# Gate matrix of a product-key expert layer: low and high gate parts accumulated in PSUM, evicted by ScalarE, weight low parts moved from GpSimd to VectorE

## Chip, core and metric

The kernel runs on one core of one Trainium2 chip. The metric is the device time of one execution in microseconds (us). A profile is one further execution under the hardware profiler; its span runs from the first to the last instruction.

## What is computed

Two transformer blocks act on 256 tokens of width 1024. The change lies in the second block's last layer, an expert layer with product keys (`peer_ffn` in the reference). Per token and head (8 heads), the top 16 of 128 scores are taken on each of two key sets, the 256 sums of pairs are ranked again, and 16 experts out of 16384 (128 x 128) remain, with softmax gates:

```
best, pos = lax.top_k(cand, PEER_TOPK)
idx = jnp.take_along_axis(cand_idx, pos, axis=-1)
g = jax.nn.softmax(best, axis=-1)
act = jax.nn.gelu(jnp.einsum('td,thkd->thk', xc, expert_u[idx]), approximate=False)
w = (g * act).astype(h.dtype)
return jnp.einsum('thk,thkd->td', w, expert_v[idx])
```

The kernel gathers nothing. It computes the activation of all 16384 experts for all tokens, multiplies by a gate matrix that is zero for experts not chosen, and multiplies by all of `expert_v`. An expert is numbered 128 i + j: i is the partition of a tile, j counts the tiles.

## The kernel before, in words

**Weights.** Every weight tile (128 x 1024, float32, 512 KB) comes by a DMA on SP's queue into `raw`; ScalarE copies it to a rounded high part `hi` (L158, L141), and VectorE or GpSimd subtracts to get the low part `lo` (L159). `plan` (from L434) lists the tiles in the order of use and says with `by` which engine subtracts: "v" is VectorE, "g" is GpSimd. Before, all 128 `eu` tiles are "g", all 128 `ev` tiles "v". `ahead(2)` keeps two tiles ready: after the matmuls of tile u, tile u+2 is fetched and split. There are three buffers each of `raw`, `hi` and `lo`.

**Two halves.** The 128 values of j are done in two halves of 64 (`JA`). In each half `experts_u` (L1698) runs 64 units; a unit is one `eu` tile: 24 matmuls of 128 x 256 (L303), 16 with `hi`, then 8 with `lo`. Every second unit, ScalarE takes a pair of activations out of PSUM (`act<-bd`, Gelu). Then `experts_v` (L1784) runs 64 `ev` tiles with matmuls of 512 columns (L1795 to L1797). `prep` (L1775) multiplies a pair of activation tiles by the gates (L1778), and ScalarE and VectorE split the result into `eh` and `el` ahead of those.

**Gates.** `gates3` (L1720) builds the gate matrix `Gt` beside `experts_u`: 32 steps of 8 tokens in each half. A step makes on VectorE a one-hot `oi` of i (L1736, 128 x 1024 in float16), a one-hot `eqj` of j (L1737, 128 x 512), and `eqj` times the gate's high and low float16 parts (`jg`, L1739, two multiplies of 128 x 512). On TensorE, for the step before, 8 matmuls (L1750, one per token, `oi` stationary, 128 moving columns: 64 of the high part, 64 of the low) fill two PSUM banks; VectorE adds the two parts with a reduce per bank (L1752) into `Gt`. In the first half, `second` (L1630) precedes the gates: the second ranking on VectorE, then for each of four (token half, key set) pairs a selection (L1678 to L1681: is_equal, multiply, reduce over 16), and two groups of transposes (L1687) with the casts to `IT`, `JT`, `GHL`.

**Order.** All engines run their instructions in program order. `weave` (L397) writes the order: after unit u of `experts_u`, it issues `CA[u]` steps of the side work in the first half (`second`, then `gates3`), `CB[u]` in the second. What is left over runs after the last unit. A gate step issues its one-hots, then the matmuls of the step before, then their eviction.

```
def prefetch():
    ...
    A(hi[:, :width], raw[:, :width], AF.Copy)
    (V if by == "v" else G).tensor_tensor(lo[:, :width], raw[:, :width], hi[:, :width].bitcast(F32), op=OP.subtract)

for i, _ in enumerate(main):
    steps(side, counts[i] if i < len(counts) else 0)
run(side)
```

Of the kernel before, what the change touches and what calls it, by code (L numbers as in the profile page):

```python
# [10 lines left out]
F16 = mybir.dt.float16  # L11
I32 = mybir.dt.int32
U32 = mybir.dt.uint32
AF = mybir.ActivationFunctionType
OP = mybir.AluOpType
# [80 lines left out]
OUTS = (4, 6, 5, 7, 2, 3, 0, 1)  # L96
JOBS = ('hf', 'gq', 'hq', 'gk', 'gv', 'lqk', 'v5', 'v2', 'sm', 'hg', 'lg', 'z', 'fq', 'fk')
LAG = (1, 1)
CA = [0] * 14 + [1] * 8 + [0, 0, 1, 0] + [1, 0] * 5 + [1, 1] + [1, 1, 2, 1] * 7
CB = [0] * 2 + [1, 0] * 28 + [1] * 6  # L100

BY_V = (0, 1)
# [9 lines left out]
def _emit(ctx, tc, I, out):  # L112
# [12 lines left out]
    def bank(tag="m"):  # L125
        if tag == "d":
            turn_["i"] += 1
            tag = turn_["d"][turn_["i"] % len(turn_["d"])]
        tag = AS.get(tag, tag)
        return ps.tile([128, 512], F32, tag=tag, name="b" + tag, bufs=BANKS[tag])  # L130
# [5 lines left out]
    def A(o, i, f, **kw):  # L136
        t = tables.get(f)
        if t and t != table[0]:
            S.preload_act_table_set(t)
            table[0] = t  # L140
        S.activation(o, i, f, **kw)  # L141
# [6 lines left out]
    def plan(*items, by="v"):  # L148
        order.extend((n, i, w, by) for n, i, w in items)
# [293 lines left out]
    plan(*[("w_out2", i, 1024) for i in range(4, 8)], by=B2)  # L443
    plan(*[("w_query", i, 1024) for i in range(16)], by="g")
    for lo_, hi_ in ((0, JA), (JA, 128)):
        plan(*[("eu", i, 1024) for i in range(lo_, hi_)], by="g")
        plan(*[("ev", i, 1024) for i in range(lo_, hi_)])

    R2 = R[:, None, :].to_broadcast([128, 2, 256])
# [1097 lines left out]

    IT = big.tile([128, 256, 2], F16)
    JT = big.tile([128, 256, 2], F16)
    GHL = big.tile([128, 2, 256, 2], F16)  # L1550
    tk = ExitStack()
    kp = tk.enter_context(tc.tile_pool(name="topk", bufs=1))
    ktmp = tk.enter_context(tc.tile_pool(name="ktmp", bufs=2))
# [76 lines left out]
    def second():  # L1630
        best = ktmp.tile([128, 2, 8, 16], F32, tag="best", name="best", bufs=1)
        pos = ktmp.tile([128, 2, 8, 16], U32, tag="pos", name="pos", bufs=1)
        for t in range(2):
            cd = ktmp.tile([128, 8, 112], F32, tag="cd", name="cd", bufs=1)
            v1, v2 = kv[:, t, 0], kv[:, t, 1]
            V.tensor_tensor(cd[:, :, 0:64].rearrange("p h (a b) -> p h a b", a=4),
                            v1[:, :, 0:4, None].to_broadcast([128, 8, 4, 16]),
                            v2[:, :, None, :].to_broadcast([128, 8, 4, 16]), op=OP.add)
            V.tensor_tensor(cd[:, :, 64:112].rearrange("p h (a b) -> p h a b", a=12),
                            v1[:, :, 4:16, None].to_broadcast([128, 8, 12, 4]),  # L1640
                            v2[:, :, None, 0:4].to_broadcast([128, 8, 12, 4]), op=OP.add)
            for h in range(0, 8, 2):
                top16(112, *((cd[:, i], best[:, t, i], pos[:, t, i]) for i in (h, h + 1)))
                yield

        ab = ktmp.tile([128, 4, 256], U32, tag="ab", name="ab", bufs=1)
        pf_ = pos.rearrange("p t h k -> p (t h k)")
        ge = ktmp.tile([128, 256], U32, tag="ge", name="ge", bufs=1)
        V.tensor_scalar(ab[:, 0], pf_, 4, None, op0=OP.logical_shift_right)
        V.tensor_scalar(ab[:, 1], pf_, 15, None, op0=OP.bitwise_and)  # L1650
        V.tensor_scalar(ab[:, 2], pf_, 2, None, op0=OP.logical_shift_right)
        V.tensor_scalar(ab[:, 3], pf_, 3, None, op0=OP.bitwise_and)
        V.tensor_scalar(ge, pf_, 6, None, op0=OP.logical_shift_right)
        abf = ktmp.tile([128, 4, 256], F32, tag="abf", name="abf", bufs=1)
        V.tensor_copy(abf, ab)
        V.tensor_scalar(abf[:, 2], abf[:, 2], 12.0, None, op0=OP.subtract)
        for i in range(2):
            V.copy_predicated(abf[:, i], ge, abf[:, 2 + i])
        abh = ktmp.tile([128, 2, 2, 8, 16], F16, tag="abh", name="abh", bufs=1)
        V.tensor_copy(abh.rearrange("p i t h k -> p i (t h k)"), abf[:, 0:2])  # L1660
        yield

        sel = ktmp.tile([128, 3, 2, 128], F32, tag="sel", name="sel", bufs=1)
        gg = sel[:, 2].rearrange("p t (h k) -> p (t h) k", h=8)
        bb = best.rearrange("p t h k -> p (t h) k")
        V.tensor_tensor(gg, bb, bb[:, :, 0:1].to_broadcast([128, 16, 16]), op=OP.subtract)
        A(gg, gg, AF.Exp)
        sm_ = ktmp.tile([128, 16], F32, tag="smk", name="smk", bufs=1)
        V.tensor_reduce(out=sm_, in_=gg, op=OP.add, axis=AX.X)
        V.reciprocal(sm_, sm_)  # L1670
        V.tensor_tensor(gg, gg, sm_[:, :, None].to_broadcast([128, 16, 16]), op=OP.mult)
        yield
        for t in range(2):
            for i in range(2):
                ixr = ktmp.tile([128, 8, 16, 16], F16, tag="ixr", name="ixr", bufs=2)
                A(ixr, kix[:, t, i, :, :, None].to_broadcast([128, 8, 16, 16]), AF.Copy)
                eq = ktmp.tile([128, 8, 16, 16], F16, tag="eq", name="eq", bufs=2)
                V.tensor_tensor(eq, abh[:, i, t, :, None, :].to_broadcast([128, 8, 16, 16]),  # L1678
                                io16[:, None].to_broadcast([128, 8, 16, 16]), op=OP.is_equal)
                V.tensor_mul(eq, eq, ixr)  # L1680
                V.tensor_reduce(out=sel[:, i, t].rearrange("p (h k) -> p h k", h=8),  # L1681
                                in_=eq.rearrange("p h a k -> p h k a"), op=OP.add, axis=AX.X)
                yield
        for t in range(2):
            p = bank("g")
            for i in range(3):
                PE.transpose(p[:, i * 128:i * 128 + 128], sel[:, i, t], ident)  # L1687
            ts = slice(t * 128, t * 128 + 128)
            two = lambda z: z[:, :, None].to_broadcast([128, 128, 2])
            V.tensor_copy(IT[:, ts], two(p[:, 0:128]))  # L1690
            V.tensor_copy(JT[:, ts], two(p[:, 128:256]))
            gs = ktmp.tile([128, 128], F32, tag="gs", name="gs", bufs=1)
            V.tensor_scalar(gs, p[:, 256:384], 4096.0, None, op0=OP.mult)
            V.tensor_copy(GHL[:, 0, ts], two(gs))
            V.tensor_sub(GHL[:, 1, ts], two(gs), GHL[:, 0, ts])
            yield

    def experts_u(j0, nj):  # L1698
# [12 lines left out]
    box = {}  # L1711
# [8 lines left out]
    def gates3(j0, nj):  # L1720


        Gt, wtmp, row = box["G"], box["w"], box["r"]

        def pairs(z, n):

            return z[:, :, None, :].to_broadcast([128, 8, n, 2])

        def along(n, j=0):
            return row[:, None, j:j + 2 * n].to_broadcast([128, 8, 2 * n]).rearrange("p t (j e) -> p t j e", e=2)  # L1730

        def one_hots(ts):
            oi = wtmp.tile([128, 8, 64, 2], F16, tag="w1", name="oi")
            jg = wtmp.tile([128, 8, 2, nj // 2, 2], F16, tag="w2", name="jg")
            eq = wtmp.tile([128, 8, nj // 2, 2], F16, tag="w3", name="eqj")
            V.tensor_tensor(oi, along(64), pairs(IT[:, ts], 64), op=OP.is_equal)  # L1736
            V.tensor_tensor(eq, along(nj // 2, j0), pairs(JT[:, ts], nj // 2), op=OP.is_equal)  # L1737
            for i in range(2):
                V.tensor_tensor(jg[:, :, i], eq, pairs(GHL[:, i, ts], nj // 2), op=OP.mult)  # L1739
            return ts, oi, jg  # L1740

        prev = None
        for t0 in range(0, 257, 8):
            new = one_hots(slice(t0, t0 + 8)) if t0 < 256 else None
            if prev:
                ts, oi, jg = prev
                for t4 in (0, 4):
                    p = bank("g").rearrange("p (t i j) -> p t i j", t=4, i=2)
                    for t in range(4):
                        PE.matmul(p[:, t, :, :nj], oi[:, t4 + t].rearrange("p a b -> p (a b)"),  # L1750
                                  jg[:, t4 + t].rearrange("p i a b -> p (i a b)"), start=True, stop=True)
                    V.tensor_reduce(out=Gt[:, :nj, ts.start + t4:ts.start + t4 + 4].rearrange("p j t -> p t j"),  # L1752
                                    in_=p.rearrange("p t i j -> p t j i")[:, :, :nj], op=OP.add, axis=AX.X)
            prev = new
            yield

# [18 lines left out]
    def prep(j):  # L1775
        wtmp = box["w"]
        w = act(j)
        V.scalar_tensor_tensor(w, w, 1.0 / 4096, box["G"][:, j:j + 2], op0=OP.mult, op1=OP.mult)  # L1778
        eh = wtmp.tile([128, 2, 256], F32R, tag="w1", name="eh")
        el = wtmp.tile([128, 2, 256], F32R, tag="w2", name="el")  # L1780
        split(w, eh, el)
        W[j] = eh, el
# [194 lines left out]
```

## Time and profile before

| | us |
|---|---|
| median of 3 runs (1574.97 to 1575.82) | 1575.59 |
| the profiled execution | 1573.7 |
| its span, first to last instruction | 1571.9 |
| mean granted TensorE clock | 0.959 |

PE is TensorE's matmuls, PEld its weight loads, DVE is VectorE, ACT ScalarE, POOL GpSimd. A row of instruction groups ends with: busy time, mean ns of one, and the engine's idle time before them with what ended it. An instruction's time on DVE or POOL includes any time in which it had started and was held up. A granted clock of 1.00 is 2.4 GHz, 0.50 is 1.2 GHz. The page cuts the span into 40 slices of 39.3 us and gives the busy share of each in tenths.

### The profile page before, as it was taken

The page shows a single profiled execution, that of the slowest core. Times are in us where ns is not written, and L with a number is a line of the kernel's source. Part 1 is how long each engine was busy: PE and PEld are TensorE (multiplying, and loading weights), DVE is VectorE, ACT ScalarE, POOL GpSimd, SP SyncE. Part 2 cuts the span into 40 slices and gives each one's busy share as a digit, 9 for nine tenths or more (in the row PEclk, how much of TensorE's full clock was granted, in tenths as well). Part 3 has the DMA queues.
Part 4 walks back from the last instruction along what each step waited for, and adds up shares of the span by engine and source line. Part 5 has one row for each costly group of instructions (what it writes and reads, how often), then busy time and mean ns, then how long its engine had stood idle before and what let it go on. Part 6 is the DMA issues. An engine that isn't in the chain of part 4 may idle for free.

```text
span 1571.9 us, 26239 instructions
## 1 busy us (share of the span) xinstructions
PE 1452.1 (92%) x10548; PEld 1323.0 (84%) x10548; DVE 1176.6 (75%) x1912; ACT 708.5 (45%) x986; POOL 582.6 (37%) x247
## 2 busy tenths in 40 slices
PE   7789898999998899979999787799999999999997
PEld 6678767999987788979998677688889999988886
DVE  4666747997783667667938999866667999976665
ACT  5623434665553345435446222244544444444444
POOL 3453212000035444866789444100007888800000
PEclk9989969999999999999999888899999999999999
DMA  6332103566544333454555332266665555556663
GB/s 217 114 94 69 55 15 113 174 200 189 185 140 132 94 95 108 153 170 136 169 183 172 106 94 94 95 189 198 192 197 179 171 172 171 168 174 191 198 194 127
DMA packets 63788, 231.35 MB, mean 147 GB/s; under 512 B 7073, under 2 KB 7602, under 8 KB 63282
## 3 DMA queue, kind: packets, MB, share of 16 engines
q1 hardware_dynamic: 62640, 226.00, 46.6%
q10 hardware_dynamic: 1026, 3.68, 0.6%
q8 instruction: 82, 1.34, 0.3%
q14 instruction: 40, 0.33, 0.1%
HBM read 228.60 MB, written 1.05 MB: 146 GB/s over the span
## 4 chain that ended last, share of the span: by engine, by line
PE 31%; DVE 21%; ACT 0%; issue 0%; DVEq 0%; ACTq 0%
PE bd L303 8%; PE bm L1796 7%; PE bm L1795 7%; PE bm L1797 7%; DVE jg L1739 7%; DVE oi L1736 5%; DVE Gt L1752 4%; DVE eqj L1737 1%; DVE sel L1681 1%; DVE eq L1680 1%; PE bn L1750 1%; DVE lo L159 0%; DVE eq L1678 0%; ACT fy L141 0%; DVE fz L1830 0%
## 5 line engine op out<-in xcount | busy, mean ns | idle before, releaser
L159 POOL TENSOR_TENSOR lo<-raw,hi 128x1024 fp32r<-128x1024 f32 x230 | 575.9, 2512 | 784.1 <-ACT hi L141 725.3
L141 ACT ACTIVATE hi<-raw 128x1024 fp32r<-128x1024 f32 x426 | 448.0, 1055 | 422.4 <-PE bd L303 234.2
L303 PE MATMUL bd<-Xh,hi 128*128 128x256 f32 (+1 forms) x1592 | 413.5, 296 | 14.1 <-ACT Xh L141 7.6
L303 PE MATMUL bd<-Xl,hi 128*128 128x256 f32 (+1 forms) x1592 | 401.7, 288 | 0.7 <-DVE Xl L240 0.7
L303 PEld LDWEIGHTS bd<-Xh,hi 128*128 128x128 f32 (+1 forms) x1592 | 313.2, 197 | 20.1 <-ACT Xh L141 7.6
L303 PEld LDWEIGHTS bd<-Xl,hi 128*128 128x128 f32 (+1 forms) x1592 | 313.0, 197 | 1.7 <-DVE Xl L240 1.0
L159 DVE TENSOR_TENSOR lo<-raw,hi 128x1024 fp32r<-128x1024 f32 x196 | 239.2, 1224 | 82.4 <-ACT hi L141 82.4
L303 PE MATMUL bd<-Xh,lo 128*128 128x256 f32 (+1 forms) x1592 | 223.6, 283 | 0.2 <-POOL lo L159 0.2
L303 PEld LDWEIGHTS bd<-Xh,lo 128*128 128x128 f32 (+1 forms) x1592 | 205.5, 191 | 0.4 <-POOL lo L159 0.4
L1795 PE MATMUL bm<-hi,eh 128*128 128x512 f32 x512 | 200.2, 391 | 3.3 <-ACT eh L141 3.3
L1796 PE MATMUL bm<-hi,el 128*128 128x512 f32 x512 | 200.2, 391 | 0.2 <-DVE el L179 0.2
L1797 PE MATMUL bm<-lo,eh 128*128 128x512 f32 x512 | 199.9, 390 | 0.0
L1739 DVE TENSOR_TENSOR jg<-eqj,GHL 128x512 f16<-128x512 f16 x128 | 130.3, 1059 | 2.2
L1795 PEld LDWEIGHTS bm<-hi,eh 128*128 128x128 f32 x512 | 96.6, 189 | 23.9 <-ACT eh L141 3.7
L1796 PEld LDWEIGHTS bm<-hi,el 128*128 128x128 f32 x512 | 96.5, 189 | 20.9 <-DVE el L179 1.0
L1797 PEld LDWEIGHTS bm<-lo,eh 128*128 128x128 f32 x512 | 96.5, 189 | 20.0
L1736 DVE TENSOR_TENSOR oi<-iorow,IT 128x1024 f16<-128x1024 f16 x64 | 96.4, 1506 | 2.4 <-PE bm L1797 2.0
L141 ACT ACTIVATE eh<-act 128x512 fp32r<-128x512 f32 x64 | 40.4, 632 | 127.0 <-DVE act L1778 127.0
L1752 DVE TENSOR_REDUCE Gt<-bn 128x256 f32<-128x512 f32 x128 | 82.0, 682 | 9.3 <-PE bn L1750 9.1
L179 DVE TENSOR_TENSOR el<-act,eh 128x512 fp32r<-128x512 f32 x64 | 44.3, 693 | 49.3 <-ACT eh L141 49.3
L1750 PE MATMUL bn<-jg,oi 128*128 128x128 f16 x512 | 44.9, 227 | 32.9 <-DVE Gt L1752 32.6
L1750 PEld LDWEIGHTS <-oi 128*128 128x128 f16 x512 | 32.6, 100 | 39.6 <-issue 26.3
(576 smaller groups left out, 2143.4 us busy)
## 6 DMA issues: line engine op xcount, KB each, us to landing
raw<-in_eu SPq DMA_DIRECT2D x128, 512.0 KB, 3.5
raw<-in_ev SPq DMA_DIRECT2D x128, 512.0 KB, 3.7
raw<-in_w_in SPq DMA_DIRECT2D x61, 512.0 KB, 3.6
raw<-in_w_up SPq DMA_DIRECT2D x44, 512.0 KB, 3.6
raw<-in_w_down SPq DMA_DIRECT2D x22, 512.0 KB, 3.7
raw<-in_w_out SPq DMA_DIRECT2D x16, 512.0 KB, 3.5
raw<-in_w_query SPq DMA_DIRECT2D x16, 512.0 KB, 3.5
raw<-in_w_ba SPq DMA_DIRECT2D x4, 512.0 KB, 3.5
```

What stands on the lines that cost most here:

```text
L141: S.activation(o, i, f, **kw)
L159: (V if by == "v" else G).tensor_tensor(lo[:, :width], raw[:, :width], hi[:, :width].bitcast(F32), op=OP.subtract)
L179: V.tensor_tensor(lo, src, hi.bitcast(F32), op=OP.subtract)
L303: PE.matmul(o, w[:, k * 128:k * 128 + M], x[:, k], start=n == 0, stop=n == 23)
L1680: V.tensor_mul(eq, eq, ixr)
L1736: V.tensor_tensor(oi, along(64), pairs(IT[:, ts], 64), op=OP.is_equal)
L1739: V.tensor_tensor(jg[:, :, i], eq, pairs(GHL[:, i, ts], nj // 2), op=OP.mult)
L1750: PE.matmul(p[:, t, :, :nj], oi[:, t4 + t].rearrange("p a b -> p (a b)"), jg[:, t4 + t].rearrange("p i a b -> p (i a b)"), start=True, sto ...
L1752: V.tensor_reduce(out=Gt[:, :nj, ts.start + t4:ts.start + t4 + 4].rearrange("p j t -> p t j"), in_=p.rearrange("p t i j -> p t j i")[:, :, ...
L1795: PE.matmul(o, eh[:, i, ts], v[0][:, n_], start=False, stop=False, skip_group_check=True)
L1796: PE.matmul(o, el[:, i, ts], v[0][:, n_], start=False, stop=False, skip_group_check=True)
L1797: PE.matmul(o, eh[:, i, ts], v[1][:, n_], start=False, stop=last and j + i == nj - 1, skip_group_check=True)
```

## The change

Four edits. (1) `eu` tiles 26 to 63 get their low part from VectorE. (2) The selection's reduce becomes four adds that halve the 16 in turn. (3) The two `jg` multiplies become one of 128 x 1024; the gate parts lie side by side per token (`GHL`, `jg` are laid out anew). (4) A gate step has 16 matmuls of 64 columns, two per token that accumulate in the same 64 columns; one PSUM bank holds 8 tokens, and one ScalarE copy evicts it, scaled by 1/4096; `prep` then needs no scale. `CA` brings the softmax step and the gate steps forward: the transposes follow units 34 and 35 instead of 36 and 37, and gate steps follow units 36 to 63 as 1, 1, 1, 1, 2.

```diff
-CA = [0] * 14 + [1] * 8 + [0, 0, 1, 0] + [1, 0] * 5 + [1, 1] + [1, 1, 2, 1] * 7
+CA = [0] * 14 + [1] * 8 + [0, 0, 1, 1] + [1, 0] * 4 + [1, 1] + [1, 1, 1, 1, 2] * 6
+UG = 26
...
-        plan(*[("eu", i, 1024) for i in range(lo_, hi_)], by="g")
+        ug = UG if lo_ == 0 else hi_
+        plan(*[("eu", i, 1024) for i in range(lo_, ug)], by="g")
+        plan(*[("eu", i, 1024) for i in range(ug, hi_)])
...
-    GHL = big.tile([128, 2, 256, 2], F16)
+    GHL = big.tile([128, 256, 2, 2], F16)
...
-                V.tensor_reduce(out=sel[:, i, t].rearrange("p (h k) -> p h k", h=8),
-                                in_=eq.rearrange("p h a k -> p h k a"), op=OP.add, axis=AX.X)
+                for w in (8, 4, 2):
+                    V.tensor_add(eq[:, :, 0:w], eq[:, :, 0:w], eq[:, :, w:2 * w])
+                V.tensor_add(sel[:, i, t].rearrange("p (h k) -> p h k", h=8), eq[:, :, 0], eq[:, :, 1])
...
-            for i in range(2):
-                V.tensor_tensor(jg[:, :, i], eq, pairs(GHL[:, i, ts], nj // 2), op=OP.mult)
+            V.tensor_tensor(jg.rearrange("p (t i) j e -> p t i (j e)", i=2),
+                            eq.rearrange("p t j e -> p t (j e)")[:, :, None].to_broadcast([128, 8, 2, nj]),
+                            pairs(GHL[:, ts].rearrange("p t i e -> p (t i) e"), h), op=OP.mult)
...
-                for t4 in (0, 4):
-                    p = bank("g").rearrange("p (t i j) -> p t i j", t=4, i=2)
-                    for t in range(4):
-                        PE.matmul(p[:, t, :, :nj], oi[:, t4 + t].rearrange("p a b -> p (a b)"),
-                                  jg[:, t4 + t].rearrange("p i a b -> p (i a b)"), start=True, stop=True)
-                    V.tensor_reduce(out=Gt[:, :nj, ts.start + t4:ts.start + t4 + 4].rearrange("p j t -> p t j"),
-                                    in_=p.rearrange("p t i j -> p t j i")[:, :, :nj], op=OP.add, axis=AX.X)
+                p = bank("g").rearrange("p (t j) -> p t j", t=8)
+                for t in range(8):
+                    for i in range(2):
+                        PE.matmul(p[:, t, :nj], oi[:, t].rearrange("p a b -> p (a b)"),
+                                  jg[:, 2 * t + i].rearrange("p a b -> p (a b)"), start=i == 0, stop=i == 1)
+                A(Gt[:, :nj, ts].rearrange("p j t -> p t j"), p[:, :, :nj], AF.Copy, scale=1.0 / 4096)
...
-        V.scalar_tensor_tensor(w, w, 1.0 / 4096, box["G"][:, j:j + 2], op0=OP.mult, op1=OP.mult)
+        V.tensor_mul(w, w, box["G"][:, j:j + 2])
```

## Rows read from the trace of the kernel before

**Rows 1.** The page: busy time by engine, and busy tenths in 40 slices.

```profile
PE 1452.1 (92%) x10548; PEld 1323.0 (84%) x10548; DVE 1176.6 (75%) x1912; ACT 708.5 (45%) x986; POOL 582.6 (37%) x247
...
PE   7789898999998899979999787799999999999997
...
DVE  4666747997783667667938999866667999976665
```

**Rows 2.** Busy time by stage: window, length, PE, PEld, DVE, ACT, POOL busy (count), clock, DMA.

```profile
752.20:826.00 73.80, 73.80 (x626) 73.80 (x626) 48.88 (x198) 34.23 (x40) 62.86 (x26) 1.00 0.59 178
...
860.50:868.60 8.10, 0.64 (x6) 0.41 (x5) 7.96 (x5) 1.54 (x2) 6.12 (x2) 0.76 0.55 161
868.60:1010.50 141.90, 108.31 (x882) 103.23 (x881) 135.58 (x206) 33.77 (x39) 56.48 (x24) 0.87 0.31 96
1186.70:1371.70 185.00, 185.00 (x1667) 183.65 (x1665) 178.22 (x170) 78.38 (x90) 152.89 (x61) 1.00 0.55 174
1371.70:1388.40 16.70, 14.17 (x130) 13.46 (x128) 15.92 (x23) 5.14 (x8) 5.02 (x2) 1.00 0.52 161
```

**Rows 3.** Timeline of TensorE's weight loads: the first unit of the first expert_v stage.

```profile
1010.50 0.29 PEld L1795 LDWEIGHTS bm<-hi,eh 128*128 128x128 f32 x1 [2.46 <-ACT eh L141]
```

**Rows 4.** Groups by form, 826 to 1010.5: VectorE's gate work.

```profile
L1736 DVE TENSOR_TENSOR oi<-iorow,IT 128x1024 f16<-128x1024 f16 x32 | 42.8, 1339 | 0.4 <-POOL iorow L1718 0.4
L1752 DVE TENSOR_REDUCE Gt<-bn 128x256 f32<-128x512 f32 x64 | 41.0, 684 | 3.9 <-PE bn L1750 3.7
...
L1737 DVE TENSOR_TENSOR eqj<-iorow,JT 128x512 f16<-128x512 f16 x32 | 15.5, 484 | 0.0
```

**Rows 5.** Waits, 826 to 1010.5: who waited for whom, total us, times, longest.

```profile
PE bn L1750 <- DVE Gt L1752: 31.1, 31, 3.4
```

**Rows 6.** Busy time around one such wait, columns as in rows 2.

```profile
879.40:885.40 6.00, 1.59 (x17) 1.19 (x16) 5.96 (x11) 0.37 (x1) 2.35 (x1) 0.98 0.60 175
885.40:888.70 3.30, 3.30 (x18) 3.30 (x17) 3.27 (x8) 0.00 (x0) 0.00 (x0) 0.52 0.03 5
```

**Rows 7.** Timeline, 961 to 972: start, us, instruction.

```profile
961.66 2.38 POOL L159 TENSOR_TENSOR lo<-raw,hi 128x1024 fp32r<-128x1024 f32 x1 [0.70 <-ACT hi L141]
...
962.36 2.22 DVE L1736 TENSOR_TENSOR oi<-iorow,IT 128x1024 f16<-128x1024 f16 x1
...
969.31 0.76 DVE L1739 TENSOR_TENSOR jg<-eqj,GHL 128x512 f16<-128x512 f16 x2
...
971.19 0.68 DVE L1736 TENSOR_TENSOR oi<-iorow,IT 128x1024 f16<-128x1024 f16 x1
```

**Rows 8.** Timeline of VectorE, 835 to 847: one selection.

```profile
835.97 1.23 DVE L1680 TENSOR_TENSOR eq<-eq,ixr 128x2048 f16<-128x2048 f16 x1 [2.66 <-ACT ixr L141]
...
843.04 3.25 DVE L1680 TENSOR_TENSOR eq<-eq,ixr 128x2048 f16<-128x2048 f16 x1
846.32 4.43 DVE L1681 TENSOR_REDUCE sel<-eq 128x128 f32<-128x2048 f16 x1
```

**Rows 9.** VectorE's low parts of weights, all 196: min/median/max ns.

```profile
L159 DVE TENSOR_TENSOR lo<-raw,hi x196: 1215/1226/1227, 7.1 to 1556.1; 128x1024 fp32r<-128x1024 f32 x196
```

**Rows 10.** Second half, line 303 alone: PE busy (count), PEld busy (count), clock, DMA.

```profile
1201.53:1368.75 167.22, 159.85 (x1296) 155.00 (x1297) 1.00 0.55 171
```

**Rows 11.** Timeline, second half, 1266 to 1270: ScalarE, and one group of gate products.

```profile
1266.67 0.58 ACT L141 ACTIVATE act<-bd 128x512 f32<-128x512 f32 x1
1268.55 1.06 ACT L141 ACTIVATE hi<-raw 128x1024 fp32r<-128x1024 f32 x1 [1.29 <-PE bd L303]
...
1269.25 0.45 PEld L1750 LDWEIGHTS <-oi 128*128 128x128 f16 x8
1269.25 0.62 PE L1750 MATMUL bn<-jg,oi 128*128 128x128 f16 x8
```

**Rows 12.** Groups by form, second half, 1195 to 1385: the gate products.

```profile
L1750 PE MATMUL bn<-jg,oi 128*128 128x128 f16 x256 | 20.2, 220 | 1.5 <-DVE Gt L1752 1.5
...
L1750 PEld LDWEIGHTS <-oi 128*128 128x128 f16 x256 | 14.6, 98 | 3.3 <-issue 1.9
```

More of the change, by code (lines that the diff above doesn't have):

```diff
@@ L1693, in second @@
             V.tensor_scalar(gs, p[:, 256:384], 4096.0, None, op0=OP.mult)
-            V.tensor_copy(GHL[:, 0, ts], two(gs))
-            V.tensor_sub(GHL[:, 1, ts], two(gs), GHL[:, 0, ts])
+            V.tensor_copy(GHL[:, ts, 0], two(gs))
+            V.tensor_sub(GHL[:, ts, 1], two(gs), GHL[:, ts, 0])
             yield
@@ L1723, in gates3 @@
         Gt, wtmp, row = box["G"], box["w"], box["r"]
+        h = nj // 2
         def pairs(z, n):
-            return z[:, :, None, :].to_broadcast([128, 8, n, 2])
+            return z[:, :, None, :].to_broadcast([128, z.shape[1], n, 2])
         def along(n, j=0):
@@ L1733, in one_hots @@
             oi = wtmp.tile([128, 8, 64, 2], F16, tag="w1", name="oi")
-            jg = wtmp.tile([128, 8, 2, nj // 2, 2], F16, tag="w2", name="jg")
-            eq = wtmp.tile([128, 8, nj // 2, 2], F16, tag="w3", name="eqj")
+            jg = wtmp.tile([128, 16, h, 2], F16, tag="w2", name="jg")
+            eq = wtmp.tile([128, 8, h, 2], F16, tag="w3", name="eqj")
             V.tensor_tensor(oi, along(64), pairs(IT[:, ts], 64), op=OP.is_equal)
-            V.tensor_tensor(eq, along(nj // 2, j0), pairs(JT[:, ts], nj // 2), op=OP.is_equal)
-            for i in range(2):
-                V.tensor_tensor(jg[:, :, i], eq, pairs(GHL[:, i, ts], nj // 2), op=OP.mult)
+            V.tensor_tensor(eq, along(h, j0), pairs(JT[:, ts], h), op=OP.is_equal)
+            V.tensor_tensor(jg.rearrange("p (t i) j e -> p t i (j e)", i=2),
+                            eq.rearrange("p t j e -> p t (j e)")[:, :, None].to_broadcast([128, 8, 2, nj]),
+                            pairs(GHL[:, ts].rearrange("p t i e -> p (t i) e"), h), op=OP.mult)
             return ts, oi, jg
```

## The prediction, made before the changed kernel was run

> **What bounds the kernel now.** The page comes first [rows 1]: TensorE is busy 92% of the span, but its slices 22 to 25, counted from 0, fall to 7 and 8 while VectorE's slices 21 to 24 stand at 8 and 9. The windows by stage place this [rows 2]. From 752 to 826 TensorE is never idle: 626 matmuls, 26 units, in 73.80 us, so a unit costs 2.838 us. From 860.5 to 868.6 it works 0.64 of 8.10 us: the second group of transposes waits for the selection. From 868.6 to 1010.5, the gate steps of the first half, it works 108 of 142 us, and VectorE 136. In the second half, 1186.7 to 1371.7, TensorE is busy all of 185.00 us. So the first half's gates are bound by VectorE, the second half's by TensorE, and a microsecond taken off VectorE is worth something in the first alone.
>
> The waits say the same: gate products waited 31.1 us for VectorE's reduce [rows 5]. A long wait costs twice. In 6.0 us TensorE worked 1.59, and for the next 3.3 us its granted clock was 0.52, about the 1.2 GHz level, though it was busy throughout [rows 6].
>
> VectorE is slow here because GpSimd holds it up. The same `oi` took 2.22 us when it began 0.70 us into a low part on GpSimd, and 0.68 us when GpSimd was quiet [rows 7]; its mean is 1.34 us [rows 4]. The selection's multiply took 3.25 us or 1.23 us [rows 8]. The reduce out of PSUM stays at 0.68 us throughout [rows 4].
>
> **The change, part by part.** I follow the stretch from 826.0, the start of unit 26, to the first expert_v matmul at 1010.5 [rows 3]: 184.5 us, 38 units.
>
> *Low parts.* 38 of them leave GpSimd, where one takes 2.4 us [rows 7], for VectorE at 1.226 us [rows 9]: 46.6 us more on VectorE. In return nothing holds it up after about 826.
>
> *Gate steps on VectorE.* Two reduces go (1.37 us a step). `oi` costs its quiet 0.68 us [rows 7], `eqj` 0.41 us (its mean of 0.48 [rows 4] still holds some hold-ups; two multiplies of the same size take 0.76 [rows 7]). The single multiply has `oi`'s 1024 elements and type, so 0.68 us; below that stands 0.62, above it 1.23, the float32 rate of [rows 9]. A step costs 1.77 us, 32 steps 56.6 us.
>
> *Selection.* is_equal and multiply cost 1.23 us each without hold-ups. The four adds have 1024, 512, 256 and 128 elements: 0.68 and at most 0.41 three times, 1.9 us in place of 4.43 [rows 8]. Four selections: 17.4 us. Softmax and casts add some 5 us. VectorE's sum is 46.6 + 56.6 + 17.4 + 5 = 125.6 us of what was 184.5, so TensorE sets the pace.
>
> *Gate products.* In the second half two units and one group of products take 167.22/27 = 6.193 us [rows 10], so a group costs 6.193 - 2 x 2.838 = 0.517 us. Its eight matmuls of 128 columns start (0.62 - 0.22)/7 = 0.057 us apart [rows 11, 12]. Sixteen of 64 columns aren't in the trace. If columns decide, one costs 0.028 us; if a matmul has a fixed price, 0.057 us. The load doesn't decide: it lasts 98 ns but follows at 0.050 us [rows 11, 12], so it hides, at least to there. I take 0.030, near the end where columns decide, since 256 columns (float32, 2.838/24) cost 0.118 us, twice what 128 cost. A group then costs 0.517 - 8 x 0.057 + 16 x 0.030 = 0.541 us, 32 of them 17.3 us.
>
> The Trainium skill, "TensorE: Matmul & The Clock Gate", section "Back-to-back issue gap", prices 1 to 64 columns at about 25 ns. By it a group would cost 0.461 us and the total be 5 us less (64 groups).
>
> *Eviction.* ScalarE gets 64 copies of 128x512 out of PSUM; its Gelu of that shape takes 0.58 us [rows 11], so 0.6 us, with 1.2 us as the upper end because `Gt` is written with a stride. ScalarE's load, two `hi` of 1.06, one Gelu and at most two copies in over 6 us, is no bound. But its queue is in order: the copy waits for the products, and the next unit's `hi` stands behind the copy. On VectorE the low part waits for that `hi`, and the next one-hots stand behind the low part. From the end of a unit this chain takes 0.54 (products) + 0.22 (their latency) + 0.6 + 1.06 + 1.23 + 1.77 = 5.4 us. After a unit with one step, TensorE needs those one-hots only 6.8 us later. After a unit with two it needs them after 0.54 + 2.84 + 0.54 = 3.9 us, so it waits 1.5 us. There are five such units: 7.5 us. The clock fell after a stretch with 4.4 of 6.0 us idle [rows 6]; I count no such loss for 1.5 us.
>
> *Start of the gates.* In units 26 to 35 VectorE has 17.4 + 12.3 (ten low parts) + 5 = 34.7 us against TensorE's 29.1; it has done some 2.5 us of this before 826 (two of the low parts). I allow 2.5 us of waits where 8.1 us stand now.
>
> *End of the half.* Now 2.46 us from last product to first expert_v [rows 3]; the copy replaces the reduce, so 2.4 us.
>
> *Sum of the stretch:* 38 x 2.838 = 107.8; transposes 0.7; products 17.3; waits 10; end 2.4: 138.2 us. Saved: 184.5 - 138.2 = 46.3 us.
>
> *Second half.* TensorE is the bound and 32 groups cost 0.024 us more each: +0.8. VectorE's reduces were hidden; only at the end, where 2.5 of 16.7 us are idle [rows 2], does their going show: -1.5. GpSimd stays here. The one multiply needs no more of VectorE than the two did, so the hold-ups, hidden now, stay hidden; ScalarE's copy delays GpSimd's next low part by some 2 us, but that part is due two units later. `prep`'s multiply keeps its shape: 0.
>
> *Total.* 1573.7 (the profiled execution, 1.8 us above its span) - 46.3 - 0.7 = 1526.7. The median of the runs lies 1.9 us above the profiled one, so 1529 us.
>
> **Rivals.**
>
> *Fixed price per matmul.* 64 columns cost 0.057 us like 128: a group costs 0.97 us, 64 x 0.43 = 27 us more, and the second half pays its part in full. 1556 us. For it: it is the only spacing measured for float16. Against: the step from 128 to 256 columns.
>
> *The multiply loses its rate.* `jg` costs 1.23 us, because one operand repeats per part and the shapes differ. First half: +0.55 x 32 on VectorE brings it to 143 us, plus waits, near 154: 16 us more. Second half: VectorE's and GpSimd's work exclude each other, and 0.41 us more than today's pair could lengthen every step, 13 us. 1558 us. Against: `oi` also reads two repeated operands and keeps its rate.
>
> *GpSimd is not the cause.* If `oi` stayed at 1.34 us and the selection's multiply at 3.25 us, VectorE would have 125.6 + 21 + 8 = 155 us, with waits some 162, 24 more than forecast: 1553 us. Against: rows 7 and 8.
>
> *Slower than before: loads no longer hide.* A stream of 0.028 us may be too short to cover a load. At 98 ns per product a group costs 0.517 - 0.456 + 1.57 = 1.63 us, 64 x 1.09 = 70 us more: 1599 us. It decides from 0.030 + 47.0/(64 x 16) = 0.076 us per product; above that the change loses. Against: loads follow each other at 0.050 us already.
>
> The same section of that page gives about 81 ns for a stream of loads and matmuls of 128 columns; held to this, the total would be 1581 us. The trace disagrees: 57 ns for such pairs.
>
> **How the numbers follow.** Forecast 0.62; fixed price 0.18; lost rate 0.06; GpSimd not the cause 0.06; loads exposed 0.05. That leaves 0.03: 0.01 for no change, 0.02 for a better case, in which the 10 us of waits vanish and columns cost 0.028 (1517 us). A measurement of this kernel tells about 0.2%, 3 us. The range goes from 1516 to 1556: the better case below, the fixed price above, with the 1.2 us copy (+0.6 for each of five waits and the end, 4 us) inside. Faster 0.94, same 0.01, slower 0.05.
>
> **What would show it.** Right: from unit 36 on TensorE near full, gate groups about 0.54 us, a wait near 1.5 us after each two-step unit and hardly any reduced clock; `oi` at 0.68 us in the first half but still about 1.7 us in the second; the stretch from unit 26 near 138 us; the second half within 3 us of now. Wrong: product spacing above 0.04 us, a longer second half, `jg` near 1.2 us, or VectorE without idle time in the first half's gates.

## The result, and the profile after

The changed kernel takes 1530.61 us (median of 4 runs, 1530.15 to 1532.70), the kernel before 1575.70 us beside it: a ratio of 0.9716 with a 95% interval of 0.9699 to 0.9733, faster. The forecast was 1529 us in a range of 1516 to 1556. The profiled execution took 1530.8 us, with a span of 1529.0 us; before it was 1571.9 us.

The page of the changed kernel, busy time by engine and the 40 slices (of 38.2 us now), answers to [rows 1].

```profile
PE 1435.1 (94%) x11060; PEld 1309.0 (86%) x11060; DVE 1002.4 (66%) x1770; ACT 766.9 (50%) x1050; POOL 478.2 (31%) x209
...
PE   6799988999997899998999899999999999999997
...
DVE  4566756998785557756944988666673334566665
```

Behind its twentieth slice TensorE now has nothing below 9 but one 8 and the last slice. VectorE's busy time fell by 174 us in total, more than the kernel gained, because most of that lay in the second half and in hold-ups. ScalarE does 58 us more.

The busy time by stage, in the columns of [rows 2], for the stretch from the start of unit 26 to the first expert_v matmul: the kernel before, the changed kernel, and the changed kernel's parts after and before the start of unit 36.

```profile
826.07:1010.50 184.43, 143.37 (x1177) 138.07 (x1175) 172.20 (x221) 60.19 (x66) 94.35 (x38) 0.89 0.36 112
...
825.34:966.28 140.94, 128.04 (x1434) 125.55 (x1432) 119.58 (x175) 88.84 (x97) 0.24 (x1) 1.00 0.45 146
...
856.50:966.28 109.78, 98.18 (x1188) 96.29 (x1186) 91.05 (x137) 67.47 (x76) 0.24 (x1) 1.00 0.45 148
825.34:856.50 31.16, 29.86 (x249) 29.26 (x248) 28.53 (x39) 21.38 (x21) 0.00 (x0) 1.00 0.45 138
```

The whole gain is here: 184.43 us became 140.94, 43.5 us less. TensorE's idle time fell from 41.1 to 12.9 us. Its busy time fell too, from 143.4 to 128.0 us, at a granted clock of 1.00 throughout, where the gate steps before had 0.87 [rows 2].

The second half, split in both kernels at the first matmul of its unit 58; the kernel before comes first:

```profile
1186.70:1365.50 178.80, 178.80 (x1610) 177.54 (x1609) 172.05 (x164) 75.77 (x87) 147.84 (x59) 1.00 0.55 174
1365.50:1388.44 22.94, 20.37 (x186) 19.57 (x185) 22.11 (x30) 7.79 (x11) 10.07 (x4) 1.00 0.53 164
...
1142.17:1322.23 180.06, 180.06 (x1826) 178.90 (x1825) 69.52 (x84) 99.77 (x113) 140.88 (x59) 1.00 0.55 171
1322.23:1343.88 21.65, 20.00 (x227) 19.59 (x225) 14.25 (x13) 13.04 (x16) 11.90 (x5) 1.00 0.60 189
```

It took 201.74 us in sum before and 201.71 us now, although VectorE works 84 us in it instead of 194. Two small changes cancel: up to unit 58 it takes 1.26 us more, from there on 1.29 us less.

The groups by form of the changed kernel, 826 to 968, answer to [rows 4]; the last row is the products'.

```profile
L142 ACT ACTIVATE Gt<-bn 128x512 f32<-128x512 f32 x32 | 35.2, 1101 | 39.2 <-PE bn L1756 39.2
L1743 DVE TENSOR_TENSOR jg<-eqj,GHL 128x1024 f16<-128x1024 f16 x32 | 22.1, 692 | 1.1
L1741 DVE TENSOR_TENSOR oi<-iorow,IT 128x1024 f16<-128x1024 f16 x32 | 21.9, 685 | 0.0
L1756 PE MATMUL bn<-jg,oi 128*128 128x64 f16 x512 | 20.5, 194 | 9.1 <-DVE jg L1743 9.1
L1742 DVE TENSOR_TENSOR eqj<-iorow,JT 128x512 f16<-128x512 f16 x32 | 13.4, 419 | 0.0
```

`oi` costs 0.685 us (1.339 before), the single multiply 0.692 us. The one surprise is the first line: ScalarE's copy takes 1.10 us. The waits of the same window come next: the 31.1 us of products waiting for a reduce [rows 5] became 9.1 us of waiting for one-hots, in six waits.

```profile
PE bn L1756 <- DVE jg L1743: 9.1, 6, 1.6
...
PEld bm L1800 <- ACT eh L142: 2.6, 1, 2.6
...
PE bd L304 <- DVE lo L160: 1.3, 3, 0.6
```

The timeline of the changed kernel around a unit with two gate steps shows the chain that the prediction described: copy, `hi`, low part, `oi`, `eqj`, `jg`, and only then the second group of products, 1.61 us late.

```profile
890.29 1.14 ACT L142 ACTIVATE Gt<-bn 128x512 f32<-128x512 f32 x1 [0.96 <-PE bn L1756]
...
891.19 1.09 ACT L142 ACTIVATE hi<-raw 128x1024 fp32r<-128x1024 f32 x1
892.31 1.23 DVE L160 TENSOR_TENSOR lo<-raw,hi 128x1024 fp32r<-128x1024 f32 x1 [0.54 <-ACT hi L142]
893.00 0.52 PEld L1756 LDWEIGHTS <-oi 128*128 128x128 f16 x16
893.01 0.64 PE L1756 MATMUL bn<-jg,oi 128*128 128x64 f16 x16
893.45 0.69 DVE L1741 TENSOR_TENSOR oi<-iorow,IT 128x1024 f16<-128x1024 f16 x1
...
894.05 0.42 DVE L1742 TENSOR_TENSOR eqj<-iorow,JT 128x512 f16<-128x512 f16 x1
894.51 0.69 DVE L1743 TENSOR_TENSOR jg<-eqj,GHL 128x1024 f16<-128x1024 f16 x1
...
895.26 0.64 PE L1756 MATMUL bn<-jg,oi 128*128 128x64 f16 x16 [1.61 <-DVE jg L1743]
```

Sixteen loads of 98 ns start within 0.52 us, (0.52 - 0.10)/15 = 0.028 us apart: a product of 64 columns costs half of one of 128. The second half's units alone, as in [rows 10], give the group's price.

```profile
1157.04:1325.52 168.48, 159.85 (x1296) 155.12 (x1296) 1.00 0.54 167
```

A step takes 168.48/27 = 6.240 us, two units of 2.838 and 0.564 us for the group; before it was 0.517.

### The profile page after: what moved, and what is told of

It reads as the page before. It is cut to its first block, busy times and chain, and to the rows that moved or that the text cites. A ratio compares the mean times of both kernels' runs of the same rounds, so it can differ in the third digit from the quotient of the medians.

```text
span 1529.0 us, 27149 instructions
## 1 busy us (share of the span) xinstructions
PE 1435.1 (94%) x11060; PEld 1309.0 (86%) x11060; DVE 1002.4 (66%) x1770; ACT 766.9 (50%) x1050; POOL 478.2 (31%) x209
## 4 chain that ended last, share of the span: by engine, by line
PE 46%; DVE 3%; ACT 1%; issue 1%; DVEq 0%
PE bd L304 21%; PE bm L1801 8%; PE bm L1802 8%; PE bm L1800 8%; PE bn L1756 2%; DVE lo L160 1%; ACT hi L142 0%; DVE eq L1685 0%; DVE jg L1743 0%; DVE eq L1683 0%; DVE oi L1741 0%; DVE eq L1681 0%; ACT fy L142 0%; DVE fz L1835 0%; DVE eqj L1742 0%
## 5 line engine op out<-in xcount | busy, mean ns | idle before, releaser
L160 POOL TENSOR_TENSOR lo<-raw,hi 128x1024 fp32r<-128x1024 f32 x192 | 471.6, 2469 | 810.6 <-ACT hi L142 520.3
L304 PE MATMUL bd<-Xh,hi 128*128 128x256 f32 (+1 forms) x1592 | 400.7, 289 | 14.3 <-ACT Xh L142 7.4
L304 PE MATMUL bd<-Xl,hi 128*128 128x256 f32 (+1 forms) x1592 | 389.8, 283 | 0.7 <-DVE Xl L241 0.7
L160 DVE TENSOR_TENSOR lo<-raw,hi 128x1024 fp32r<-128x1024 f32 x234 | 285.5, 1224 | 138.2 <-ACT hi L142 138.2
L304 PEld LDWEIGHTS bd<-Xl,hi 128*128 128x128 f32 (+1 forms) x1592 | 302.8, 190 | 1.7 <-DVE Xl L241 1.0
L1741 DVE TENSOR_TENSOR oi<-iorow,IT 128x1024 f16<-128x1024 f16 x64 | 60.9, 951 | 115.6 <-PE bn L1756 113.6
L142 ACT ACTIVATE Gt<-bn 128x512 f32<-128x512 f32 x64 | 71.0, 1109 | 104.1 <-PE bn L1756 104.1
L1743 DVE TENSOR_TENSOR jg<-eqj,GHL 128x1024 f16<-128x1024 f16 x64 | 52.8, 825 | 2.2
L1756 PE MATMUL bn<-jg,oi 128*128 128x64 f16 x1024 | 41.0, 194 | 9.1 <-DVE jg L1743 9.1
L1783 DVE TENSOR_TENSOR act<-act,Gt 128x512 f32<-128x512 f32 x64 | 43.9, 685 | 1.2 <-ACT Gt L142 1.2
```

The costliest lines, as they stand in the source:

```text
L304: PE.matmul(o, w[:, k * 128:k * 128 + M], x[:, k], start=n == 0, stop=n == 23)
L1743: V.tensor_tensor(jg.rearrange("p (t i) j e -> p t i (j e)", i=2), eq.rearrange("p t j e -> p t (j e)")[:, :, None].to_broadcast([128, 8, ...
L1756: PE.matmul(p[:, t, :nj], oi[:, t].rearrange("p a b -> p (a b)"), jg[:, 2 * t + i].rearrange("p a b -> p (a b)"), start=i == 0, stop=i == 1)
L1783: V.tensor_mul(w, w, box["G"][:, j:j + 2])
```

## The experiments

Totals vary by several us from run to run, and the profiles show where: unit 26 starts anywhere from 820 to 832 us, after stages that no kernel here alters but the two with spread in their label, whose units 21 to 25 take 14.20 us as in the others. The two expert_v stages vary as well, by 2.7 and 1.7 us. The stretch from unit 26 to the first expert_v matmul is therefore read from each profile beside the total: 184.4 us before, 140.9 us changed. It repeats well: second_v below, whose edit leaves this stretch as it is, took 140.93 us in it. Ratios are to the kernel before on the same chip (changed: 0.9716).

The expected totals start from 1530.6 us, measured where the kernel before took 1575.7 us. In the runs below the kernel before took 1569.7 to 1573.1 us, and eight of the eleven totals lie below their expected range. Taken by ratio (times 1575.7 us), only lows_alone and reduce_back miss it by more than 2.5 us.

**All `eu` low parts back on GpSimd** (label lows_back).

```diff
-UG = 26
+UG = 64
```

> The changed kernel, but all 128 eu low parts are on GpSimd again; everything else stays as changed. Theory (GpSimd's low parts hold VectorE up, so VectorE and GpSimd must share the time): from unit 26 on, 38 x 2.4 us on GpSimd and some 75 us of float16 work on VectorE exclude each other, 166 us and more against 140.9 us now, so 1553 to 1560 us, and oi is stretched to 1.3 us or more again. Rival (what bound VectorE was its own work, above all the reduces that the change takes away): VectorE keeps only some 80 us of its own in 141 us, so no loss, 1531 us or 1 to 2 us less.

Measured: 1551.65 us, ratio 0.9871 (0.9846 to 0.9897). Its stage row, and the groups by form there:

```profile
823.98:983.75 159.77, 134.61 (x1434) 132.03 (x1432) 136.46 (x136) 88.06 (x96) 96.31 (x38) 0.94 0.41 129
```

```profile
L1741 DVE TENSOR_TENSOR oi<-iorow,IT 128x1024 f16<-128x1024 f16 x32 | 40.1, 1254 | 13.4 <-PE bn L1756 13.0 <-POOL iorow L1722 0.4
...
L1685 DVE TENSOR_TENSOR eq<-eq 128x1024 f16<-128x1024 f16 x4 | 6.9, 1730 | 0.1
...
L1685 DVE TENSOR_TENSOR eq<-eq 128x256 f16<-128x256 f16 x4 | 5.3, 1334 | 0.1
```

The waits of TensorE there:

```profile
PE bn L1756 <- DVE jg L1743: 12.9, 5, 3.2
...
PE bn L1691 <- DVE sel L1686: 9.8, 3, 3.8
```

The rival falls: 18.8 us come back with no work added to VectorE. TensorE waits for VectorE's selection and one-hots, and never for a low part from GpSimd. `oi` is at 1.25 us again, and an add of 256 elements takes 1.33 us. The stretch is some 6 us shorter than the 166 us that were expected. Durations were summed there, which overcounts (see the next run); whether the two engines also exclude each other less strictly was not separated.

**Only the low parts moved** (label lows_alone): the kernel before with the four changed `plan` lines.

```diff
+UG = 26
-        plan(*[("eu", i, 1024) for i in range(lo_, hi_)], by="g")
+        ug = UG if lo_ == 0 else hi_
+        plan(*[("eu", i, 1024) for i in range(lo_, ug)], by="g")
+        plan(*[("eu", i, 1024) for i in range(ug, hi_)])
```

> The kernel before with one part of the change: eu tiles 26 to 63 get their low part from VectorE; reduces, two multiplies, order stay. Theory: VectorE's own work is then 46.6 (low parts) + 105 (32 steps of 0.68 + 0.41 + 0.82 + 1.37) + 27 (selection) + 5 = 184 us, as long as the stretch is now; hold-ups are gone but low parts and reduces fill their place, so 1570 to 1585 us. Rival (the hold-ups are the whole cost of the stretch): they sum to about 43 us, and taking them away gives some 1535 us.

Measured: 1563.65 us, ratio 0.9937 (0.9916 to 0.9958).

```profile
831.74:1006.71 174.97, 141.87 (x1177) 137.42 (x1175) 168.17 (x259) 60.22 (x66) 0.24 (x1) 0.90 0.37 118
```

```profile
L1739 DVE TENSOR_TENSOR oi<-iorow,IT 128x1024 f16<-128x1024 f16 x32 | 21.9, 683 | 0.0
```

9.5 us of the stretch's 43.5. The hold-ups are gone (`oi` takes its quiet 0.683 us), yet VectorE is busy 168 of 175 us: the low parts and reduces fill the place. The rival, by which the hold-ups alone were the cost, falls. The theory's 184 us were too many by 16, and the total fell 6 us below its range. Summed durations overcount: the groups of this stretch, count times mean, add up to 185 us, while the window, which counts each microsecond once, has 168. Successive instructions on VectorE overlap a little.

**Products of 128 columns, reduce and two multiplies back** (label reduce_back): the kernel before with the new `plan`, `CA` and the selection's adds; lines L1739 to L1752 and L1778 as before.

> The kernel before with the low parts on VectorE from unit 26, the selection's four adds and the new order, but with eight products of 128 columns, the reduce on VectorE and two multiplies as before. Theory (the reduce costs VectorE 1.37 us a step, and VectorE has no room for it): VectorE's sum is 125.6 + 44 + 4.5 = 174 us for the stretch, which becomes about 178 us against 140.9, so 1560 to 1570 us. Rival (TensorE and ScalarE set the pace, the reduce would be hidden): 1531 us, or less, as ScalarE's copy no longer stands ahead of hi.

Measured: 1552.93 us, ratio 0.9881 (0.9856 to 0.9906).

```profile
821.93:984.84 162.91, 139.41 (x1178) 134.84 (x1176) 157.96 (x271) 59.21 (x65) 0.24 (x1) 0.92 0.39 126
```

22.0 us come back, with VectorE busy 158 of 163 us. The rival falls; the size was again overcounted by some 15 us, for the same reason (the durations add up to 175 us).

**The selection's reduce back** (label sel_back).

```diff
-                for w in (8, 4, 2):
-                    V.tensor_add(eq[:, :, 0:w], eq[:, :, 0:w], eq[:, :, w:2 * w])
-                V.tensor_add(sel[:, i, t].rearrange("p (h k) -> p h k", h=8), eq[:, :, 0], eq[:, :, 1])
+                V.tensor_reduce(out=sel[:, i, t].rearrange("p (h k) -> p h k", h=8),
+                                in_=eq.rearrange("p h a k -> p h k a"), op=OP.add, axis=AX.X)
```

> The changed kernel with the selection's reduce in place of the four adds. Theory (VectorE is full from unit 26 to 36, so its work there turns into waits): four reduces of 4.4 us instead of adds of 1.7 us, 10.9 us more, of which 8 to 11 us show: 1538 to 1542 us, with TensorE waiting for the transposes' inputs and a reduced clock after it. Rival (VectorE catches up, since it has slack later): at most 2 us, 1530 to 1533 us.

Measured: 1539.19 us, ratio 0.9796 (0.9763 to 0.9830). Its stage row and its waits:

```profile
823.97:974.39 150.42, 131.02 (x1434) 128.37 (x1432) 129.41 (x163) 88.84 (x97) 0.24 (x1) 0.98 0.43 137
```

```profile
PE bd L304 <- DVE lo L160: 8.9, 4, 2.9
```

9.5 us come back, nearly all of the added work: VectorE is busy 9.8 us longer (10.9 were expected). TensorE waits, however, for units' low parts (1.3 us in the changed kernel), which stand behind the reduces, not for the transposes as expected.

**The copy walks tokens inside** (label evict_rows).

```diff
-                A(Gt[:, :nj, ts].rearrange("p j t -> p t j"), p[:, :, :nj], AF.Copy, scale=1.0 / 4096)
+                A(Gt[:, :nj, ts], p.rearrange("p t j -> p j t")[:, :nj], AF.Copy, scale=1.0 / 4096)
```

> The changed kernel, with ScalarE's copy walking j outside and tokens inside: it writes runs of 8 adjacent float32 and reads PSUM with a step of 64, instead of reading in a row and writing with a step of 256. Theory (the write with a stride makes the copy cost 1.10 us, where 0.58 to 0.6 were expected): the copy falls to about 0.65 us, each of the five waits at units with two steps falls from 1.6 to about 1.1 us, and the end of the half by 0.45 us: 1527 to 1528.5 us. Rival (the strided read costs the same, or the copy's price is not the stride): copy at 1.1 us or more, 1530.6 us or slower.

Measured: 1525.73 us, ratio 0.9691 (0.9669 to 0.9713). Its stage row, its copies (min/median/max ns) and its waits:

```profile
827.63:965.98 138.35, 128.04 (x1433) 125.54 (x1431) 119.51 (x175) 75.20 (x97) 0.24 (x1) 1.00 0.47 149
```

```profile
L142 ACT ACTIVATE Gt<-bn x64: 597/598/601, 866.5 to 1337.7; 128x512 f32<-128x512 f32 x64
```

```profile
PE bn L1756 <- DVE jg L1743: 6.9, 6, 1.2
```

The stride of the write is the cause: 1.10 us become 0.598 although the read of PSUM is strided now, and the stretch loses 2.6 us. The second half loses 0.4 us (201.30). The stretch ends at 138.35 us, where the prediction, with a copy of 0.6 us, had put 138.2; how far that is luck, the next section says.

**Side work five units earlier, never two steps in a unit** (label spread).

```diff
-CA = [0] * 14 + [1] * 8 + [0, 0, 1, 1] + [1, 0] * 4 + [1, 1] + [1, 1, 1, 1, 2] * 6
-UG = 26
+CA = [0] * 9 + [1] * 8 + [0, 0, 1, 1] + [1, 0] * 4 + [1, 1] + [1] * 33
+UG = 21
```

> The changed kernel with the side work five units earlier, so that every unit from 31 to 63 carries one gate step and none carries two; low parts on VectorE from unit 21. Theory (a unit with two steps makes TensorE wait 1.5 to 1.6 us for one-hots that stand behind copy, hi and low part; a unit with one step doesn't): five such waits go, 8 us, and VectorE idles before unit 26 anyway: 1522 to 1524 us. Rival (VectorE's sum in the stretch sets it, and waits come back elsewhere): less than 3 us gained, 1528 to 1531 us.

Measured: 1520.98 us, ratio 0.9669 (0.9648 to 0.9689). Its stage row and its wait for one-hots:

```profile
829.40:960.87 131.47, 127.37 (x1434) 125.44 (x1432) 112.56 (x161) 82.70 (x93) 0.24 (x1) 1.00 0.51 161
```

```profile
PE bn L1756 <- DVE jg L1743: 1.2, 1, 1.2
```

The five waits, 8.0 us, are gone, and the stretch is 9.5 us shorter; TensorE is busy 127.4 of 131.5 us. The work that moved ahead costs nothing where it went: units 21 to 25 take 14.20 us with it and without.

**Both** (label spread_rows), `evict_rows` and `spread` together.

> Both: side work five units earlier and ScalarE's copy walking tokens inside. If the copy falls to 0.65 us and single steps leave TensorE no wait, what is left of the copy is the end of the first half: 0.5 us below the kernel with the earlier side work alone, 1521.5 to 1523.5 us. If the strided read costs as much as the strided write: the same as with the earlier side work alone.

Measured: 1517.72 us, ratio 0.9641 (0.9621 to 0.9662), the lowest median here. The stretch is 131.03 us: 0.4 us from the copy's end, as expected. The total is 3.3 us below that of spread, where 0.5 us was expected; the stretch and the second half give 0.8 of it, and the rest lies in the stages whose times scatter.

**The second half's low parts on VectorE too** (label second_v).

```diff
-        ug = UG if lo_ == 0 else hi_
+        ug = UG if lo_ == 0 else lo_
```

> The changed kernel with the second half's 64 eu low parts on VectorE too. Theory (the second half is bound by TensorE, whose low parts are due two units later, so hold-ups there cost nothing): within 2 us of the changed kernel, 1528.5 to 1532.5 us, although oi falls from about 1.2 to 0.68 us there. Rival (GpSimd costs time wherever it runs beside VectorE): 5 us or more faster, 1525 us or less.

Measured: 1530.09 us, ratio 0.9729 (0.9706 to 0.9753). Its second half:

```profile
1141.28:1342.99 201.71, 200.06 (x2051) 198.49 (x2049) 128.72 (x162) 112.20 (x129) 0.00 (x0) 1.00 0.53 171
```

To the hundredth 201.71 us as with GpSimd, with `oi` at 0.684 us instead of 1.231 and 45 us more of VectorE's time. Neither the hold-ups nor the added low parts cost anything where TensorE is the bound.

**The copy on VectorE** (label v_evict).

```diff
-                A(Gt[:, :nj, ts].rearrange("p j t -> p t j"), p[:, :, :nj], AF.Copy, scale=1.0 / 4096)
+                V.tensor_scalar(Gt[:, :nj, ts].rearrange("p j t -> p t j"), p[:, :, :nj], 1.0 / 4096, None, op0=OP.mult)
```

> The changed kernel with the eviction of the gate products on VectorE (one multiply by 1/4096 per step, 128x512 out of PSUM) instead of ScalarE. Theory (VectorE has little room in the first half's gates): some 0.6 us a step more there, 19 us over 32 steps, of which VectorE's idle time can take some 12; the copy also leaves the way of hi, but the eviction stands ahead of the next low part on VectorE itself: 1535 to 1545 us, second half unchanged. Rival (the waits come from ScalarE's queue alone): with the copy out of ScalarE's queue the five waits shrink, 1522 to 1527 us.

Measured: 1537.54 us, ratio 0.9787 (0.9760 to 0.9814). Its stage row and its copy, by form:

```profile
821.74:973.50 151.76, 134.18 (x1434) 131.15 (x1432) 146.16 (x207) 59.25 (x65) 0.24 (x1) 0.95 0.42 136
```

```profile
L1758 DVE TENSOR_SCALAR Gt<-bn 128x512 f32<-128x512 f32 x32 | 34.2, 1067 | 1.0 <-PE bn L1756 1.0
```

The stretch is 10.8 us longer, but VectorE's copy took 1.07 us, not 0.6. So this run alone doesn't tell load from stride; the next does.

**The copy on VectorE, tokens inside** (label v_evict_rows), the two edits joined.

> The eviction on VectorE, but walking tokens inside, so that it writes runs of 8. It tells whether the 10.8 us that the eviction on VectorE cost in the first half's stretch (151.8 against 140.9 us) were its load or its strided write. If it was the strided write (1.07 us for 0.6): the copy falls to about 0.6 us, the stretch by some 0.47 x 32 x 0.7 = 10 us to 139 to 143 us, near ScalarE's own 140.9 and a little above the 138.4 that ScalarE has with the same order of walking: 1525 to 1532 us. If it was the load and its place in VectorE's queue: the stretch stays above 146 us, 1534 us or more.

Measured: 1524.27 us, ratio 0.9706 (0.9687 to 0.9726). Its stage row and its copy, by form:

```profile
820.66:962.01 141.35, 129.55 (x1433) 127.05 (x1431) 136.60 (x207) 59.30 (x65) 0.24 (x1) 0.99 0.47 145
```

```profile
L1758 DVE TENSOR_SCALAR Gt<-bn 128x512 f32<-128x512 f32 x32 | 21.9, 685 | 0.1
```

10.4 of the 10.8 us were the stride. With runs of 8 written, VectorE (busy 137 of 141 us) can just carry the copy, and with that order of walking ScalarE's eviction is worth 141.35 - 138.35 = 3.0 us.

**Two multiplies again** (label two_mults).

```diff
-            V.tensor_tensor(jg.rearrange("p (t i) j e -> p t i (j e)", i=2),
-                            eq.rearrange("p t j e -> p t (j e)")[:, :, None].to_broadcast([128, 8, 2, nj]),
-                            pairs(GHL[:, ts].rearrange("p t i e -> p (t i) e"), h), op=OP.mult)
+            for i in range(2):
+                V.tensor_tensor(jg.rearrange("p (t i) j e -> p t i j e", i=2)[:, :, i], eq,
+                                pairs(GHL[:, ts, i], h), op=OP.mult)
```

> The changed kernel with two multiplies of 128x512 per step instead of one of 128x1024. Theory (the multiply counts only where TensorE waits for one-hots): two cost some 0.13 us more than one, which shows in the five waits and at the start: 0.7 to 1 us longer in the stretch of the first half, within the spread of the total: 1529.5 to 1533 us; second half unchanged. Rival (VectorE sets the pace throughout): 0.13 x 32 = 4 us more, 1534 us or above.

Measured: 1525.32 us, ratio 0.9708 (0.9681 to 0.9734); the stretch is 141.23 us, 0.3 us longer, and the second half is 201.71 us again. The ratio agrees with the changed kernel's; in the profiles, unit 26 began at 820 us here and at 825 us there, which is where the totals differ. The rival falls; the single multiply is worth some 0.3 us.

## Why the prediction was right

The mechanism and the place were right, point by point, while two terms were mis-sized and the closeness of some figures is luck.

- *What bounds.* VectorE bound the first half's gates and TensorE the second half's. Up to unit 58 of the second half VectorE works 103 us less and the kernel gained nothing (178.80 to 180.06 us); in second_v it works 45 us more at no cost.
- *GpSimd holds VectorE up.* Shown by lows_back (18.8 us) and by `oi` at 0.685 us without GpSimd.
- *No part does it alone.* Taken back one at a time, the low parts cost 18.8, products with reduce, copy and multiplies 22.0, the selection 9.5 us: 50.3 in sum for a gain of 43.5. Moved alone, the low parts gained 9.5. With the reduces still on it, VectorE has no room for the low parts. The new order of the steps was not taken back by itself.
- *Products.* 0.030 us was taken, 0.028 measured. The fixed-price and exposed-load rivals fall, and so does the lost rate, with the one multiply at 0.692 us.
- *Waits.* 10 us were allowed. The five two-step units made 8.0 us and the first group of products 1.2 (the six waits of 9.1 us), and TensorE waited 1.3 us for low parts: 10.4 in all.
- *The end of the second half.* -1.5 us were forecast for it. From unit 58 on it is 1.29 us shorter (22.94 to 21.65), with the dearer groups in it.

Two terms were mis-sized. The first is the gate group, which came out at 0.564 instead of 0.541 us: what it costs beside its products rose from 0.517 - 8 x 0.057 = 0.06 to 0.564 - 16 x 0.028 = 0.12 us, which the step had held fixed. That is 0.7 us in each half. In the second half it is nearly all of the error: the 27 groups up to unit 58 cost 0.047 us more each, 1.26 us, where 0.024 each were forecast.

The second is the copy. It was put at 0.6 us, with 1.2 us as the upper end because of the strided write; it took 1.10 us. evict_rows shows its price in the stretch, 2.6 us. The Trainium skill's page "SBUF — State Buffer", section "Door 1: The DMA port swizzle", says that float32 accesses which leave a 16-byte line each time pay a penalty; these runs agree (1.10 us for single elements 1 KB apart, 0.598 us for runs of 8).

Three agreements are in part luck. The sum for the stretch had 125.8 us of work (units, transposes, products) and 12.4 us of waits and end; TensorE was busy 128.0 us and idle 12.9. With the copy that the sum assumed (evict_rows), it is busy 128.0 us and idle 10.3, so two errors of some 2 us cancel in its 138.35 us. Likewise the wait after a two-step unit was forecast at 1.5 us and measured at 1.6 with a copy that is 0.5 us longer than assumed; in evict_rows it is 1.2 us. What the chain had left out is the overlap of its instructions: in the timeline above it takes 4.91 us from the start of the copy (890.29) to the end of `jg` (895.20), while the six durations add up to 5.26.

The total is the third. 46.3 + 0.7 us of gain were forecast and 43.5 + 0.0 measured, so 3.5 us of gain are missing. The profiled execution, forecast at 1526.7 us, took 1530.8, that is 4.1 us more; the other 0.6 us lie in the stages that scatter. The forecast then added 1.9 us, because the median of the kernel before lay that much above its profiled execution. In the changed kernel it lies 0.2 us below, and so 1529 us is missed by only 1.6 us.

One sign did not come: `oi` was to stay at about 1.7 us in the second half, and it fell to 1.235 us there, from 1.705 before.

```profile
L1741 DVE TENSOR_TENSOR oi<-iorow,IT 128x1024 f16<-128x1024 f16 x31 | 38.3, 1235 | 115.1 <-PE bn L1756 113.6 <-PE bm L1802 1.5
```

So the hold-ups did not stay as they were; why was not tried, and second_v shows that they cost no time there.

VectorE's sum of 125.6 us was 119.6 us by the window; it mattered little there, but summed durations misled the expectations of lows_alone and reduce_back by some 15 us.

## What to carry to other kernels

When one engine's share of the work must shrink, sum its busy time for the stretch with the change in it: moving the low parts onto VectorE paid 9.5 us alone and 18.8 us together with the reduces that left it. Look in an in-order chain for the instruction that everything else stands behind (here copy, `hi`, low part, one-hots), and write the order so that no unit needs its end twice; that was worth 9.5 us more. When an eviction has to turn its data, let the inner loop write adjacent elements and the read from PSUM take the stride: here that was 1.10 against 0.598 us.

## What the runs showed of the hardware that was not expected

- A strided float32 write (single elements 1 KB apart) is dear for both ScalarE and VectorE: 1.10 us against 0.598, and 1.07 us against 0.685, for 128x512 out of PSUM. Reading PSUM with a step of 64 elements shows no price on ScalarE: 0.598 us, where its Gelu of that shape, which reads in a row, takes 0.593.
- Beside GpSimd, every add of the selection's chain took some 1.03 us longer, whatever its length: 1.73 us against 0.69 for 128x1024 in float16, 1.33 us against 0.29 for 128x256. The four adds together took 5.8 us in lows_back, more than the reduce that they replace (4.25 us in the kernel before).
- TensorE takes a new 128x128 float16 load with every product of 64 columns at 0.028 us, half the price of 128 columns. Sixteen such products cost 0.12 us beside their own time between two streams of float32 matmuls, eight of 128 columns 0.06 us; why was not tried.
